# The first mixer's and the memory's products as single fp32 matmuls, without high and low parts

## The chip, the cores and the metric

The kernel runs on one core of one Trainium2 chip. The metric is the device time of one execution in microseconds (us). The core's engines are TensorE (PE, with its weight loads as PEld), VectorE (DVE), ScalarE (ACT), GpSimd (POOL) and SyncE (SP), which here issues the DMAs. Each works through its own queue in order and waits on semaphores for the others. TensorE's clock has two levels, 1.2 and 2.4 GHz; the profile gives the granted clock as a share of the full one.

## What is computed

A decoder trunk of two layers on 512 tokens of width 1024, in fp32. Layer 0's mixer ("mixer A") scores earlier keys with a light indexer, keeps the top 128 of them for each query, and attends to these. In both layers four more heads attend to 256 memory tokens.

```python
proj = rms_norm(x, norm_mix) @ w_in            # q, k, v, qi, ki, wi, qm of mixer A
logits = einsum('bqhd,bsd->bqhs', qi, ki)
score = einsum('bqhs,bqh->bqs', relu(logits), wi)
_, idx = top_k(score, n_sel)                   # n_sel = 128
# softmax attention of q over the kept k, v (12 query heads, 4 key heads, rotary)
kv = rms_norm(mem, norm_mem) @ w_mem_kv        # both layers
# softmax attention of qm over the memory's keys and values
x = x + concat([mix, mo]) @ w_out
x = x + swiglu_ffn(rms_norm(x, norm_ffn))
```

Layer 1 has another mixer (dilated windows), and a final norm ends the kernel.

## The kernel before

Activations lie transposed, 128 features by 512 tokens to a tile, eight such tiles (KT = 8) for the width of 1024. A product takes a weight tile of 128 output columns and accumulates eight matmuls of 128x128 weights by 512 tokens in one PSUM bank.

Each of the large products is made in three parts. The operands are split into a high part in fp32r, a format of reduced precision, and a low part, the rest (`_split2`, L48 on ACT and L51 on DVE or POOL). For each k there are three matmuls: high by high, low by high, high by low (`projs` L225 to L227, `proj_steps` L213 to L215, `token_major` L403 to L405 for values, which lie token by token in 256 columns, `scores` L414 for the attention's score products, which take 64 rows a head and so run a pair of heads in the two halves of the array). The weights come through `load` (L176) into `wf`, a ring of two buffers of 1 MB with two weight tiles each; `wsplit` makes `wh` and `wl` of them (three buffers each), so that a `wf` buffer is free as soon as its tiles are split. `prep` (L309, L310) makes the split input `xh`, `xl`. Small products are plain fp32: `row` (L268) spreads the reciprocal roots along the tokens, `pv` (L385) multiplies probabilities by values with the two heads of a pair in the two column halves of the array, and the transposes (L427).

Only PE's order is written by hand, in the order of the code; a scheduler orders the other engines when the program is built, and that order is fixed. `layer0` issues on PE: the indexer's key and first query tile together, three more index queries, then (woven, `_weave`) the first key tile and the values with the index logits of four head pairs and three query blocks each; then the memory's row, the second key tile, two memory queries, the memory's keys and values (`memory_kv`), memory attention woven with four query tiles, and the sparse attention in 18 units, into which the last two query tiles, layer 1's memory products (`memory_ahead`) and the output projection are filled. The logits go through ReLU on ACT into SBUF (L756) and are summed up on DVE (L758, L760). The top-k (`topk`) is sixteen rounds on DVE, each with a maximum (L695) and a replacement (L696) for three query blocks, and masks at the end (L700). Memory attention reduces its scores on DVE (L555), which ACT's exponential then needs. The memory's squares are summed on POOL (`memory_squares`, L282, L294); `ssq_cols` and `rsqrt_cols` (L234 to L243, a chain of thirteen small DVE steps) make the reciprocal roots of them, and `row` spreads these (DVE L266, PE L268).

```python
for k in range(KT):                                     # proj_steps, before
    s = slice(k * 128, (k + 1) * 128)
    mm(out, wh[:, s], xh[k], start=k == 0, stop=False)
    mm(out, wh[:, s], xl[k], start=False, stop=False)
    mm(out, wl[:, s], xh[k], start=False, stop=k == KT - 1)
```

## Time and profile before

| | us |
|---|---|
| median of 3 timed runs | 1280.42 (1276.65 to 1281.71) |
| profiled execution | 1287.35 |
| its span, first to last instruction | 1285.6 |
| PE busy | 1218.7 (95%) |
| weight loads (PEld) busy | 983.7 (77%) |
| DVE busy | 586.0 (46%) |
| ACT busy | 498.7 (39%) |
| POOL busy | 389.4 (30%) |
| mean granted TensorE clock | 0.973 |

The profiled execution is one of its own, a little longer than the median. By the chain of work that ended last, PE holds 81% of the span and DVE 12%. A busy share is an average over stages with different limits: the feed-forward parts, which fill most of the span, keep PE busy almost without a gap, while the first quarter of the span has many. A record's duration includes the way through the array, so the pace of matmuls is read from one start to the next.

### The profile page before, as it was taken

How to read it: one execution, taken by the hardware profiler on the slowest of the kernel's cores; microseconds unless marked ns; L12 is line 12 of the kernel's file. 1: busy time of each engine (PE TensorE's matmuls, PEld its weight loads, DVE VectorE, ACT ScalarE, POOL GpSimd, SP SyncE). 2: the span in 40 equal slices, each digit the busy share in tenths (PEclk: the TensorE clock that was granted, in tenths of full speed). 3: DMA queues.
4: the chain of work that ended last, by engine and by line, in shares of the span. 5: the costliest groups of instructions: out<-in, count | busy, mean ns of one | idle time of the engine just before them, and what ended most of it. 6: DMA issues, size and time to landing. Idle time of an engine off the chain costs nothing.

```text
span 1285.6 us, 14958 instructions
## 1 busy us (share of the span) xinstructions
PE 1218.7 (95%) x5868; PEld 983.7 (77%) x5868; DVE 586.0 (46%) x1054; ACT 498.7 (39%) x859; POOL 389.4 (30%) x242
## 2 busy tenths in 40 slices
PE   6688979999999999999998999999999999999997
PEld 5467657677888888888886779887788888888886
DVE  7789976548333333322224542548533333331212
ACT  6564666525323322322223764534332233222222
POOL 4637464244222122212222322333322221121222
PEclk9789999999999999999998999989899999999998
DMA  5402132212222222222233111211222222222221
GB/s 179 131 33 101 49 113 72 70 36 97 78 88 97 98 99 98 78 90 90 90 111 107 66 66 34 97 35 41 92 98 89 80 94 98 99 90 90 91 90 66
DMA packets 30214, 109.98 MB, mean 86 GB/s; under 512 B 2495, under 2 KB 12095, under 8 KB 21695
## 3 DMA queue, kind: packets, MB, share of 16 engines
q1 hardware_dynamic: 29598, 108.50, 24.1%
q8 instruction: 46, 0.75, 0.2%
q10 hardware_dynamic: 544, 0.52, 0.1%
q14 instruction: 26, 0.20, 0.0%
HBM read 105.74 MB, written 3.28 MB: 85 GB/s over the span
## 4 chain that ended last, share of the span: by engine, by line
PE 81%; DVE 12%; DMA 3%; issue 1%; ACT 1%; POOL 1%; SPq 0%; DVEq 0%; ACTq 0%; POOLq 0%
PE psS L226 5%; PE psS L225 5%; PE psS L227 5%; PE psT L225 3%; PE psT L227 3%; PE psT L226 3%; PE psacc L225 3%; PE psacc L226 3%; PE psacc L227 3%; PE psacc L200 3%; PE psS L414 3%; PE psS L200 3%; PE psS L202 3%; PE psS L201 3%; PE psacc L202 3%; PE psacc L201 3%
## 5 line engine op out<-in xcount | busy, mean ns | idle before, releaser
L51 POOL TENSOR_TENSOR wl<-wf,wh 128x1024 fp32r<-128x1024 f32 x98 | 238.5, 2434 | 684.6 <-ACT wh L48 621.8
L48 ACT CAST wh<-wf 128x1024 fp32r<-128x1024 f32 (+1 forms) x178 | 183.6, 1032 | 527.9 <-issue 171.3
L51 DVE TENSOR_TENSOR wl<-wf,wh 128x1024 fp32r<-128x1024 f32 (+1 forms) x95 | 118.5, 1247 | 94.1 <-ACT wh L48 94.1
L225 PE MATMUL psS<-xh,wh 128*128 128x512 f32 x296 | 120.0, 405 | 6.8 <-ACT wh L48 6.8
L227 PE MATMUL psS<-xh,wl 128*128 128x512 f32 x296 | 119.2, 403 | 2.8 <-DVE wl L51 2.8
L226 PE MATMUL psS<-xl,wh 128*128 128x512 f32 x296 | 118.9, 402 | 2.8 <-DVE xl L310 2.8
L225 PE MATMUL psT<-xh,wh 128*128 128x512 f32 x200 | 81.1, 405 | 0.0
L227 PE MATMUL psT<-xh,wl 128*128 128x512 f32 x200 | 80.7, 403 | 0.0
L226 PE MATMUL psT<-xl,wh 128*128 128x512 f32 x200 | 80.7, 403 | 0.0
L225 PE MATMUL psacc<-xh,wh 128*128 128x512 f32 x192 | 77.3, 403 | 0.0
L226 PE MATMUL psacc<-xl,wh 128*128 128x512 f32 x192 | 76.9, 401 | 0.0
L227 PE MATMUL psacc<-xh,wl 128*128 128x512 f32 x192 | 76.9, 400 | 0.0
L225 PEld LDWEIGHTS psS<-xh,wh 128*128 128x128 f32 x296 | 56.8, 192 | 20.5 <-ACT wh L48 6.8
L227 PEld LDWEIGHTS psS<-xh,wl 128*128 128x128 f32 x296 | 56.7, 191 | 17.2 <-DVE wl L51 4.2
L226 PEld LDWEIGHTS psS<-xl,wh 128*128 128x128 f32 x296 | 56.8, 192 | 16.7 <-DVE xl L310 3.3
L294 POOL TENSOR_TENSOR ssq<-ssq,t 128x512 f32<-128x512 f32 (+1 forms) x34 | 50.8, 1493 | 55.1 <-ACT t L284 53.9
L213 PE MATMUL psacc<-xh,wh 128*128 128x512 f32 x144 | 62.9, 437 | 0.0
L652 DVE TENSOR_TENSOR raw<-psacc,R 128x512 f32<-128x512 f32 x22 | 15.2, 691 | 103.1 <-PE psacc L227 103.1
L215 PE MATMUL psacc<-xh,wl 128*128 128x512 f32 x144 | 58.1, 404 | 0.0
L214 PE MATMUL psacc<-xl,wh 128*128 128x512 f32 x144 | 58.0, 403 | 0.0
L339 POOL TENSOR_TENSOR raw<-raw,table 128x512 f32<-128x512 f32 x21 | 26.9, 1283 | 72.7 <-ACT raw L336 54.9
L627 DVE TENSOR_TENSOR xT<-xT,psacc 128x512 f32<-128x512 f32 x44 | 30.1, 686 | 38.7 <-PE psacc L202 38.6
(335 smaller groups left out, 2812.7 us busy)
## 6 DMA issues: line engine op xcount, KB each, us to landing
wf<-in_gu SPq DMA_DIRECT2D x44, 1024.0 KB
wf<-in_dn SPq DMA_DIRECT2D x16, 1024.0 KB
wf<-in_in SPq DMA_DIRECT2D x13, 1024.0 KB
wf<-in_dn SPq DMA_DIRECT2D x16, 384.0 KB
wf<-in_v SPq DMA_DIRECT2D x3, 1024.0 KB
xT<-in_x SPq DMA_DIRECT2D x8, 256.0 KB
wf<-in_mk SPq DMA_DIRECT2D x2, 1024.0 KB
wf<-in_mv SPq DMA_DIRECT2D x2, 1024.0 KB
```

The source lines that it names most:

```text
L48: nc.scalar.copy(hi, src)
L51: lo_engine.tensor_tensor(out=lo, in0=src, in1=hi.bitcast(F32), op=ALU.subtract)
L200: mm(out, wh[k], xh[k], start=first and k == 0, stop=False)
L201: mm(out, wh[k], xl[k], start=False, stop=False)
L202: mm(out, wl[k], xh[k], start=False, stop=last and k == n - 1)
L213: mm(out, wh[:, s], xh[k], start=k == 0, stop=False)
L214: mm(out, wh[:, s], xl[k], start=False, stop=False)
L215: mm(out, wl[:, s], xh[k], start=False, stop=k == KT - 1)
L225: mm(out, wh[:, s], xh[k], start=k == 0, stop=False)
L226: mm(out, wh[:, s], xl[k], start=False, stop=False)
L227: mm(out, wl[:, s], xh[k], start=False, stop=k == KT - 1)
L294: engine.tensor_tensor(out=parts[part], in0=parts[part], in1=sq, op=ALU.add)
```

## The change

- The input of the first mixer is scaled once on DVE (`scaled`), without a split; the memory is scaled once on ACT (`memory_scaled`). The weights are used straight from `wf` (`plain_chunks`, and `load` alone for values). The products of the first mixer, except its output projection, and the memory's products of both layers take one fp32 matmul for each k (`fp32_steps`, `fp32_tokens`).
- Index queries and keys, queries, keys and memory queries and keys are kept whole, so their score products take one fp32 matmul a head instead of three in fp32r. `rope` and `plain` no longer split their result; in `rope_steps` POOL now does the multiplications.
- ReLU of the logits is done in place in PSUM, and the logits use the banks of two tags in turn.
- `angles` moves behind the first products. `memory_squares` moves behind the first key step, and `ssq_cols` of the memory behind the logits and values. `row` of the memory and its scaling move behind the second key tile.
- `memory_ahead` uses the memory that is still in SBUF and doesn't load it again; what it keeps in DRAM for layer 1 is halved for the keys.

```diff
+    def plain_chunks(self, name, order):
+        src = self.io[name]
+        for a in range(0, len(order), 2):
+            m = min(2, len(order) - a)
+            w = self.load(src[order[a]:order[a] + m].rearrange("t p n -> p t n"), [m, KT * 128])
+            for j in range(m):
+                yield w[:, j]
+    def fp32_steps(self, out, w, x):
+        for k in range(KT):
+            self.nc.tensor.matmul(out, w[:, k * 128:(k + 1) * 128], x[k], start=k == 0, stop=k == KT - 1)
+            if k % 2:
+                yield 1
+    def fp32_tokens(self, out, w, ks, x, b):
+        n = out.shape[-1]
+        for k in ks:
+            self.nc.tensor.matmul(out, x[k][:, b], w[:, k * n:(k + 1) * n], start=k == 0, stop=k == KT - 1)
...
+    def scaled(self, gi):
+        ...
+            nc.vector.tensor_scalar(t, self.xT[:, k], self.gains[:, gi, k:k + 1], None, op0=ALU.mult)
+            add(self.xT[:, k], 0, nc.vector)
...
         mm = self.nc.tensor.matmul
+        if units[0][2] is None:
+            for out, q, _, k, _, rows, qs, ks in units:
+                mm(out, q[rows, qs], k[rows, ks], start=True, stop=True)
+            return
         for a in range(3):
...
     def layer0(self):
-        self.angles()
-        xh, xl, parts = self.prep(0, early=4, squares=(1, 3))
-        first = [self.wsplit(self.first[j], nc.vector) for j in range(2)]
+        x, parts = self.scaled(0)
...
         cols = self.ssq_cols(parts)
+        self.angles()
...
         index_q(1, p1)
-        mem_parts = self.memory_squares(mem)
...
-                ps = [self.psum("S") for _ in range(2)]
-                self.scores([(ps[s][:, :n], qih, qil, kih, kil, slice(s * 64, s * 64 + 64), q, slice(0, n))
+                tag = ("S", "acc")[(j + i) % 2]
+                ps = [self.psum(tag) for _ in range(2)]
+                self.scores([(ps[s][:, :n], qi, None, ki, None, slice(s * 64, s * 64 + 64), q, slice(0, n))
                              for s in range(2)])
                 for s in range(2):
-                    t = self.tmp(("t", "o")[s])
+                    t = ps[s]
-                    self.mark = nc.scalar.activation(t[:, :n], ps[s][:, :n], AF.Relu)
+                    nc.scalar.activation(t[:, :n], t[:, :n], AF.Relu)
...
-        def rope_steps(dst, *out, tag="acc", mul=None):
+        def rope_steps(dst, out, tag="acc"):
             p = self.psum(tag)
-            yield from self.proj_steps(p, next(ws), xh, xl)
-            dst.append(self.rope(p, cs, sn, *out, add=nc.gpsimd, split=nc.gpsimd, mul=mul))
+            yield from self.fp32_steps(p, next(ws), x)
+            dst.append(self.rope(p, cs, sn, out, None, add=nc.gpsimd, mul=nc.gpsimd))
...
         next(steps)
-        self.mem_cols = self.ssq_cols(mem_parts, n=2, keep=True)
+        mem_parts = self.memory_squares(mem)
         every = itertools.chain.from_iterable(logits(j) for j in range(4))
         _weave(itertools.islice(steps, 12), every, nb=1)
-        self.mem_row = self.row(self.mem_cols, 2, dst=self.cst.tile([128, MEM], F32, name="mem_row"))
-        mem = self.memory_split(0, mem)
         for _ in steps:
             pass
-        for _ in rope_steps(K, kb[:, 2], kb[:, 3], tag="T", mul=nc.gpsimd):
+        self.mem_cols = self.ssq_cols(mem_parts, n=2, keep=True)
+        for _ in rope_steps(K, kb[:, 1], tag="T"):
             pass
+        self.mem_row = self.row(self.mem_cols, 2, dst=self.cst.tile([128, MEM], F32, name="mem_row"))
+        xm = self.memory_scaled(0, mem)
```

The change also moves instructions. In the rows that follow a line number is that of the kernel the rows are from.

PE before, in the first key tile's steps, ahead of the first logits: the matmul of the memory's squares (`ssq`), from which the reciprocal roots come, stands between two of the key's matmuls (`psO`).

```order
L214 MATMUL psO<-xl,wh 128x512
L215 MATMUL psO<-xh,wl 128x512
L256 MATMUL psacc<-ones,ssq 128x2 x2
L213 MATMUL psO<-xh,wh 128x512
```

PE now, from the last logits (`ki`, `qi`) to the first scores of memory attention (`km`, `qm`): `xg` is the scaled input, `mg` the scaled memory.

```order
L440 MATMUL psacc<-ki,qi 128x384 x2
L440 MATMUL psS<-ki,qi 128x512 x2
L278 MATMUL psacc<-ones,ssq 128x2 x2
L207 MATMUL psT<-xg,wf 128x512 x8
L290 MATMUL psacc<-raw,ones 128x256
L207 MATMUL psacc<-xg,wf 128x512 x16
L207 MATMUL psacc<-mg,wf 128x256 x16
L215 MATMUL psacc<-wf,mg 128x256 x16
L440 MATMUL psS<-km,qm 128x256 x4
```

The matmul of the squares moved behind the last logits, and only the second key tile (x8) now stands between it and the row's matmul (L290).

DVE before, in the first logits' sums: the last steps of the memory's reciprocal roots (`rs_q`, `rs_keep`) and the multiplication that makes the row's operand of them (L266).

```order
L242 SCALAR_TENSOR_TENSOR rs_q<-rs_v,rs_q 128x2
L758 TENSOR_SCALAR score<-t,wi 128x256
L243 SCALAR_TENSOR_TENSOR rs_keep<-rs_q,rs_keep 128x2
L760 SCALAR_TENSOR_TENSOR score<-o,wi,score 128x256
L758 TENSOR_SCALAR score<-t,wi 128x384
L760 SCALAR_TENSOR_TENSOR score<-o,wi,score 128x384
L340 TENSOR_TENSOR raw<-raw 128x512
L333 TENSOR_TENSOR raw<-psO,table 128x512
L266 TENSOR_SCALAR raw<-ident,rs_keep 128x128 x2
```

DVE now, behind the last logits' sums: the same chain, with the first top-k round (`m_` are its maxima).

```order
L261 TENSOR_SCALAR rs_keep<-rs_i 128x2
L263 TENSOR_TENSOR rs_q<-rs_keep 128x2
L709 MAX m_900<-score 128x8
L709 MAX m_903<-score 128x8
L709 MAX m_906<-score 128x8
L264 SCALAR_TENSOR_TENSOR rs_q<-rs_v,rs_q 128x2
L710 MATCH_REPLACE score<-m_900,score 128x512
L710 MATCH_REPLACE score<-m_903,score 128x384
L710 MATCH_REPLACE score<-m_906,score 128x256
L265 SCALAR_TENSOR_TENSOR rs_keep<-rs_q,rs_keep 128x2
```

And DVE now, where the chain ends: the row's operand (L288) in the fifth round.

```order
L265 SCALAR_TENSOR_TENSOR rs_keep<-rs_q,rs_keep 128x2
L709 MAX m_936<-score 128x8
L709 MAX m_939<-score 128x8
L709 MAX m_942<-score 128x8
L288 TENSOR_SCALAR raw<-ident,rs_keep 128x128 x2
L710 MATCH_REPLACE score<-m_936,score 128x512
```

The chain moved from among the logits to among the top-k, where four rounds and three maxima stand ahead of its end.

DVE before, in the middle of the top-k: two reductions of memory attention (L555) stand between the maxima of one round.

```order
L695 MAX m_1545<-score 128x8
L555 TENSOR_REDUCE nm<-psS 128x2 x2
L695 MAX m_1548<-score 128x8
L695 MAX m_1551<-score 128x8
L127 TENSOR_SCALAR o<-o 128x128
L696 MATCH_REPLACE score<-m_1545,score 128x512
```

DVE now, at the end of the top-k: the last round's replacements, the masks (L714), and then the first reductions (L569).

```order
L710 MATCH_REPLACE score<-m_1035,score 128x512
L710 MATCH_REPLACE score<-m_1038,score 128x384
L710 MATCH_REPLACE score<-m_1041,score 128x256
L714 TENSOR_SCALAR score<-score 128x512
L714 TENSOR_SCALAR score<-score 128x384
L714 TENSOR_SCALAR score<-score 128x256
L569 TENSOR_REDUCE nm<-psS 128x2 x4
L486 RECIPROCAL den<-den 128x8
L449 COPY pt<-psT 128x2x256 x2
```

All reductions of memory attention moved from within the top-k to behind it.

## Rows read from the trace of the kernel before

**Rows 1.** By stage: length, PE, PEld, DVE, ACT, POOL busy, clock, DMA share, GB/s
```profile
0.00:48.43 48.43, 36.27 (x134) 27.65 (x135) 33.13 (x53) 27.49 (x43) 20.46 (x17) 0.96 0.53 173
48.43:96.71 48.28, 34.88 (x197) 26.37 (x196) 42.86 (x62) 29.23 (x58) 27.67 (x22) 0.79 0.16 56
96.71:131.15 34.44, 30.36 (x172) 26.83 (x171) 33.83 (x82) 14.39 (x22) 23.88 (x19) 0.95 0.33 121
131.15:171.20 40.05, 36.97 (x201) 25.97 (x200) 40.05 (x102) 25.59 (x60) 22.68 (x15) 1.00 0.14 45
171.20:301.89 130.69, 121.70 (x721) 90.82 (x721) 78.93 (x190) 68.90 (x173) 57.15 (x38) 0.97 0.20 70
```

**Rows 2.** Timeline, PE: start, us, operation, records [idle before, releaser]; fp32 among fp32r
```profile
318.66 1.02 PE L268 MATMUL psacc<-raw,ones 128*128 128x512 f32 x2
319.12 0.79 PE L225 MATMUL psS<-xh,wh 128*128 128x512 f32 x1
319.75 0.40 PE L226 MATMUL psS<-xl,wh 128*128 128x512 f32 x1
319.98 0.40 PE L227 MATMUL psS<-xh,wl 128*128 128x512 f32 x1
```

**Rows 3.** Timeline, PE: products of 256 columns in fp32r
```profile
214.32 0.28 PE L404 MATMUL psacc<-wh,ml 128*128 128x256 f32 x1
214.44 0.28 PE L405 MATMUL psacc<-wl,mh 128*128 128x256 f32 x1
```

**Rows 4.** Timeline, PE: fp32 on column halves; a pair of scores and what follows
```profile
146.49 1.94 PE L385 MATMUL psO<-pt,vm 128*64 128x512 f32 x8
...
217.69 0.50 PE L414 MATMUL psS<-k,qh 64*128 64x512 f32 x2
...
218.59 1.73 PE L385 MATMUL psO<-pt,v 128*64 128x512 f32 x8
```

**Rows 5.** Timeline, PE: waits of the first two stages
```profile
6.83 0.79 PE L225 MATMUL psS<-xh,wh 128*128 128x512 f32 x1 [6.83 <-ACT wh L48]
...
12.47 0.79 PE L227 MATMUL psS<-xh,wl 128*128 128x512 f32 x1 [2.02 <-DVE wl L51]
...
34.28 1.12 PE L268 MATMUL psacc<-raw,ones 128*128 128x512 f32 x2 [2.56 <-DVE raw L266]
...
59.58 1.01 PE L256 MATMUL psacc<-ones,ssq 128*128 128x2 f32 x4 [9.61 <-POOL ssq L294]
```

**Rows 6.** Timeline, SP: issues of two weight loads
```profile
37.28 1.31 SPq L176 DMA_DIRECT2D wf<-in_vw  x1
...
95.39 0.37 SPq L176 DMA_DIRECT2D wf<-in_mk  x1
```

**Rows 7.** Timeline, ACT: the value weights' first use
```profile
48.20 1.05 ACT L48 CAST wh<-wf 128x1024 fp32r<-128x1024 f32 x1 [0.69 <-DMA wf<-in_vw]
```

**Rows 8.** Timeline, POOL: first of the memory's squares; the first table behind them
```profile
43.64 0.61 POOL L282 TENSOR_TENSOR ssq<-mem 128x256 f32<-128x256 f32 x1 [11.74 <-DMA mem<-in_mem]
...
59.48 1.74 POOL L373 TENSOR_TENSOR table<-raw,R 128x512 f32<-128x512 f32 x1
```

**Rows 9.** Timeline, DVE: two rounds of the top-k, a memory key, the masks
```profile
101.61 1.48 DVE L695 MAX8 m<-score 128x8 f32<-128x512 f32 x3 [0.40 <-POOL score L762]
...
104.59 1.47 DVE L695 MAX8 m<-score 128x8 f32<-128x512 f32 x3
...
119.62 0.42 DVE L362 SCALAR_TENSOR_TENSOR t<-psacc,mem_row 128x256 f32<-128x256 f32 x1
...
167.90 4.22 DVE L700 TENSOR_SCALAR score<-score 128x512 f32<-128x512 f32 x3
```

**Rows 10.** Timeline, DVE: one of the reciprocal root's small steps
```profile
32.16 0.16 DVE L241 TENSOR_TENSOR rs_q<-rs_y 128x4 f32<-128x4 f32 x1
```

**Rows 11.** Short stretches, columns as in rows 1: after a stop; during a load
```profile
60.00:66.00 6.00, 6.00 (x19) 4.45 (x20) 5.30 (x6) 3.59 (x7) 6.00 (x5) 0.50 0.27 70
...
96.00:100.00 4.00, 4.00 (x19) 3.04 (x20) 3.90 (x4) 1.50 (x4) 3.20 (x3) 1.00 0.71 265
```

More of the change, by code (lines that the diff above doesn't have):

```diff
@@ L315, in prep @@
         return xh, xl, parts
-    def rope_proj(self, w, xh, xl, cs, sn, hi, lo, any_bank=False, by_residue=False):
-        p = self.psum_any() if any_bank else self.psum("acc")
-        self.proj(p, w, xh, xl)
-        return self.rope(p, cs, sn, hi, lo, by_residue)
+    def scaled(self, gi):
+        nc = self.nc
+        xg = []
+        add, parts = self.squares()
+        for k in range(KT):
+            if k % 4 == 0:
+                big = self.big("xg", F32)
+            t = big[:, (k % 4) * S:(k % 4 + 1) * S]
+            nc.vector.tensor_scalar(t, self.xT[:, k], self.gains[:, gi, k:k + 1], None, op0=ALU.mult)
+            add(self.xT[:, k], 0, nc.vector)
+            xg.append(t)
+        return xg, parts
     def rope(self, p, cs, sn, hi, lo, by_residue=False, mul=None, add=None, split=None, twice=None):
@@ L339, in rope @@
         (mul or nc.gpsimd).tensor_tensor(out=sw, in0=sw, in1=sn, op=ALU.mult)
-        (add or nc.vector).tensor_tensor(out=raw, in0=raw, in1=sw, op=ALU.add)
+        last = hi if lo is None and twice is None else raw
+        (add or nc.vector).tensor_tensor(out=last, in0=raw, in1=sw, op=ALU.add)
         if twice is not None:
-            nc.vector.tensor_tensor(out=raw, in0=raw, in1=twice, op=ALU.mult)
+            nc.vector.tensor_tensor(out=hi, in0=raw, in1=twice, op=ALU.mult)
+        if lo is None:
+            return hi
         if by_residue:
@@ L514, in memory_ahead @@
+            t = self.slot("vm", F32)[:, :256]
+            self.values(p, self.mem_cols[:, i:i + 1], t)
+            yield t
+    def memory_ahead(self, mem):
         nc = self.nc
-        mem = self.load(self.io["mem"].rearrange("(k p) n -> p k n", p=128), [KT, MEM])
-        m = self.memory_split(1, [mem[:, k] for k in range(KT)])
-        self.kept = self.dram.tile([4, 128, 512], F32, name="kept")
+        x = self.memory_scaled(1, mem)
+        self.kept = self.dram.tile([4, 128, 256], F32, name="kept")
@@ L518, in memory_ahead @@
         n = 0
-        for r in self.memory_kv(1, m):
-            if r:
-                n_cols = 512 if n < 2 else 256
-                nc.sync.dma_start(self.kept[n][:, :n_cols], r[1].bitcast(F32)[:, :n_cols])
+        for r in self.memory_kv(1, x):
+            if r is not None:
+                nc.sync.dma_start(self.kept[n], r)
                 n += 1
@@ L526, in memory_back @@
     def memory_back(self):
-        ts = []
-        for n in range(4):
-            ts.append(self.slot("kept", F32R if n < 2 else F32))
-            n_cols = 512 if n < 2 else 256
-            self.nc.sync.dma_start(ts[n].bitcast(F32)[:, :n_cols], self.kept[n][:, :n_cols])
-        self.mem_kv = [(t[:, :MEM], t[:, MEM:]) for t in ts[:2]], ts[2:]
+        ts = [self.slot("kept", F32)[:, :256] for _ in range(4)]
+        for n, t in enumerate(ts):
+            self.nc.sync.dma_start(t, self.kept[n])
+        self.mem_kv = ts[:2], ts[2:]
     def memory_attention(self, qm, early):
@@ L703, in layer0 @@
         nc, mm = self.nc, self.nc.tensor.matmul
-        self.angles()
-        xh, xl, parts = self.prep(0, early=4, squares=(1, 3))
-        first = [self.wsplit(self.first[j], nc.vector) for j in range(2)]
+        x, parts = self.scaled(0)
         pk, pq = self.psum("S"), self.psum("S")
-        self.projs([(pk, first[0]), (pq, first[1])], xh, xl)
-        ws = itertools.chain(self.chunks("in0", [2, 3]), self.chunks("in0", [4, 5]),
-                             self.chunks("in0", list(range(6, 15)), lo=("gpsimd", "gpsimd")))
+        for k in range(KT):
+            for p, w in zip((pk, pq), self.first):
+                mm(p, w[:, k * 128:(k + 1) * 128], x[k], start=k == 0, stop=k == KT - 1)
+        ws = itertools.chain(self.plain_chunks("in0", [2, 3]), self.plain_chunks("in0", [4, 5]),
+                             self.plain_chunks("in0", list(range(6, 15))))
         def product(tag="T"):
             p = self.psum(tag)
-            self.proj(p, next(ws), xh, xl)
+            for _ in self.fp32_steps(p, next(ws), x):
+                pass
             return p
         cols = self.ssq_cols(parts)
+        self.angles()
         ci, si = (self.angle_table(1, sine, self.slot("table", F32)) for sine in (False, True))
@@ L873, in layer0 @@
         outs = list(self.mem_out)
-        fill = itertools.chain(queries(2), self.memory_ahead())
+        fill = itertools.chain(queries(2), self.memory_ahead(mem))
         for u in range(-ahead, nu + 4):
```

98 lines of the change are left out of this document (34 added, 64 removed).

## Prediction

> **What bounds the kernel now.** I read the table by stage first, then PE's timeline inside the first stages for its waits, then DVE's and POOL's timelines for who ends them. The change touches only the first mixer (the first 301.89 us of the span) and layer 1's short memory attention, so five stages matter: A to 48.43 (indexer products), B to 96.71 (index logits woven with key and value products), C to 131.15 (second keys, memory queries, memory's keys and values), D to 171.20 (memory attention woven with four queries), E to 301.89 (sparse attention) [rows 1]. In A and B PE stands idle or at low clock: in B it is busy 34.88 of 48.28 us at a mean granted clock of 0.79. In C and D it is DVE that is full: 33.83 of 34.44 us and 40.05 of 40.05; that is the top-k, with everything else threaded through it. E is PE's. So the change has to be costed on PE in A, B and E, and on DVE's queue in C and D.
>
> **What one product costs.** Before, a product of 512 columns is three matmuls 0.23 us apart, 0.70 us. The trace holds plain fp32 matmuls too: the one that spreads a row enters PE at 318.66 as two records; the next matmul's record is stretched (0.79 instead of 0.40 us), and the one after starts at 319.75, so its own place was 319.75 - 0.23 = 319.52 [rows 2]. A plain fp32 product therefore takes 0.86 us, 0.16 more than the three it replaces. At 256 columns three at 0.115 us are 0.35 [rows 3]; half of 0.86 is 0.43: 0.08 more. So the change makes PE's work longer and takes work from ACT, DVE and POOL.
>
> Score products of 64 rows go in pairs, one head in each half of the array. A pair at 512 columns takes 0.90 us with three passes; eight fp32 records of 512 columns on the two column halves take 1.94 us, where four products one by one would take 3.44, so fp32 runs two at a time there [rows 4]. No fp32 product on row halves is shown. Lower bound: two at a time, one pass more, +0.23 us per 512 columns; upper bound: one head after the other, a further 0.86. In units of 512 columns B has 9 pairs (4 x (256+384+512)), D 4, E 15, layer 1 another 4. I take the lower bound, since the halves of the other kind are the nearest row: +2.1, +0.9, +3.5, +0.9 us.
>
> The Trainium skill (Perfetto Trace Analysis, Engine Utilization) halves TensorE's rate for FP32_LOW_HIGH; read as the price of a whole product, that would be 0.47 us and a saving. The row shows each of the two records at half rate, so the trace agrees by record and not by product; by the rule the time would be that of the first rival.
>
> **Stage A.** Five products of eight: 40 x 0.16 = +6.4. The first product no longer waits for the weight's cast (1.0 us), the next not for its low part (2.02), and the reciprocal root no longer for a DVE that splits (2.56) [rows 5]; the low clock that follows costs half of (1 - 0.96) x 2 x 48.43 = 3.9 us, 1.9. The load of tiles 4 and 5 now waits until the first products are through with their buffer, and stands behind the memory loads on SP; the load that stood there before was issued at 37.28 and used at 48.20 [rows 6, 7]. I give it 1.3. Sum +0.2.
>
> **Stage B.** The 13.4 us of idle go: 9.61 of them wait for the memory's squares [rows 5], whose product moves behind the logits. B's work at full clock is 24 x 0.23 + 96 x 0.115 + logits 9 x 0.90 + 1.0 for small ones = 25.6 us against 34.88 busy, so slow clock is another 9.3. New work: 8 x 0.16 + 32 x 0.08 = 3.8, logits 2.1. New waits: index query 3 is multiplied on POOL behind the fifteen memory squares and two tables (43.64 to 59.48 us for the squares alone, perhaps 7 us earlier now [rows 8]), and its sum on DVE stands ahead of the first logit's: PE comes to the third logit some 4 us early. A wait for the last banks (1.5) and slow clock after them (2). 48.28 - 13.4 - 9.3 + 5.9 + 7.5 = 39.0: -9.3.
>
> **Stage C, where the sign is decided.** Call T0 the moment when PE's matmul for the memory's root stands behind the last logits. In DVE's new order the root's steps alternate with top-k rounds, and the row product's operand comes after four rounds and three maxima (order rows in the section on the change). A round takes 104.59 - 101.61 = 2.98 us [rows 9], a root step 0.2 [rows 10]. So: 2.5 for the last logits on ACT, DVE and POOL, 4 x 2.98 + 1.4 + 9 x 0.2 + 0.4 = 15.5: the operand is there at T0 + 18. PE has 8 x 0.86 = 6.9 us of second keys for that time and then stands for 10.8 us; behind the waiting matmul all its queue stands, the memory queries first. Then: 0.3, memory queries 16 x 0.86 = 13.8, slow clock after the stop 2.5 (after the 9.6 us stop 60 to 66 us ran at 0.50 [rows 11]), memory keys 16 x 0.43 = 6.9. The memory's value weights take the key weights' buffer, because the other holds a query tile still to come; formerly the split copies freed it early, now only the last product does. A load of 1 MB issued at 95.39 had moved by 100 [rows 6, 11]: 4.9 with the issue, and 1.7 of slow clock; values 6.9. Together T0 + 55.
>
> DVE says the same by itself: in its new order all sixteen rounds stand ahead of the first reduction of memory attention. 2.5 + 16 x 2.98 + 13 x 0.2 + 0.4 + 0.8 + the three masks: T0 + 55 if these take 1.2 us without POOL beside them, T0 + 58 at the 4.2 us they took [rows 9]. The two memory keys' multiplications are the 0.8 (0.42 each) [rows 9]. Even if PE's stops vanished, memory attention could not start earlier. C: 55 - 34.4 = +20.6, bounds +17 and +25. Formerly C and D overlapped with the top-k; now D follows it.
>
> **Stage D.** 32 x 0.16 = 5.1 and scores 0.9; DVE is free, so 2 of the 3.1 us of idle go: +4.0. **Stage E.** Queries 16 x 0.16 = 2.6, layer 1's memory products 32 x 0.08 = 2.6, scores 3.5; 5 of 9.0 us of idle go (the memory's low parts and casts no longer stand on DVE), and 2 of slow clock (0.97): +1.7. **Layer 1** scores +0.9, less splitting of its memory queries hidden under PE: +0.9. The two feed-forward parts and layer 1's products stay as they are.
>
> **Sum.** +0.2 - 9.3 + 20.6 + 4.0 + 1.7 + 0.9 = +18.1. The profiled execution took 1287.35 us (span 1285.6), so 1305.5 by its own time; the three timed runs have a median of 1280.42, and I forecast 1280.4 + 18.1 = 1299 us rounded up, 1.4% slower. Errors of some 4 us in B, C and E each give the forecast itself about 1284 to 1314.
>
> **Rivals.**
> - *Faster: the two records of a product follow at fp32r's pace (0.47 us).* Against the forecast a product of 512 columns is then 0.39 cheaper, one of 256 0.20, a score pair 0.46. A: 40 x 0.39 = 15.6, of which the load of tiles 4 and 5 holds some 12 back, so -3.7. B: 3.1 + 6.4 + 4.1, of which the POOL chain holds 5 back, so -18. C keeps its +20.6, since DVE's queue sets it. D: 12.5 + 1.8, so -10. E: 6.2 + 6.4 + 6.9, so -18. Layer 1 -1. Sum -30: 1250. The row at 318.66 speaks against it [rows 2]. A, B, D and E hold 96 products of 512 and 64 of 256 columns, so it takes the sign from 0.86 - 18.1 / 128 = 0.72 us a product downwards. Chance 0.06.
> - *No change: C keeps its length.* If the root's steps and memory attention's reductions got through while the top-k runs, C would stay near 35 and the sum be -2.5: 1278. DVE's queue runs in its order and the order is fixed at build, which speaks against it; that logits could end earlier than I sum them speaks for it. Chance 0.10.
> - *Slower still: fp32 score pairs on row halves run one head after the other.* 32 x 0.86 = +27.5: 1326. Column halves speak against it; nothing shows it excluded. Chance 0.12.
> - That the change doesn't do what it says: the splits are gone from ACT, DVE and POOL by the order, so no chance is kept for it.
>
> **How the numbers follow.** The forecast has 0.70, other causes 0.02. A measurement tells about 0.5%, 6.4 us, from no change. Of the forecast's 0.70 about 0.09 lies within that. Slower 0.61 + 0.12 = 0.73; same 0.10 + 0.09 = 0.19; faster 0.06 + 0.02 = 0.08. The range reaches from the no-change rival with its error (1277) to just past the score rival (1328); left out are the first rival and the tails, about 0.15.
>
> **What would show it.** In the profile after: two records per product 0.43 us apart (0.86 a product); DVE full with the top-k without a break, PE idle by 8 to 13 us before the memory's row product and about 5 before the memory's value products, the first reduction of memory attention behind the masks; B shorter by about 8 us. It is wrong if the row product doesn't wait, if a product takes 0.70 us or less, or if B ends as late as before.

## Result and the profile after

The changed kernel takes 1297.06 us (median of 4 runs, 1296.31 to 1298.61) against 1280.45 us (4 runs, 1276.65 to 1281.71): a ratio of 1.0136, 95% interval 1.0113 to 1.0159. It is slower by 1.4%, as forecast (1299). The profiled execution took 1297.15 us, span 1295.4. Of the kernels below, one execution each of *root_early* (1731.91 us) and *late_split_relu_sbuf* (1707.64 us) ran at a mean granted clock of 0.65 and is left out of their medians.

By stretch, in the profiled executions (before: [rows 1]; "rest" is everything from the first feed-forward product on):

| stretch | before | forecast | after | difference |
|---|---|---|---|---|
| A | 48.43 | +0.2 | 46.91 | -1.5 |
| B | 48.28 | -9.3 | 40.49 | -7.8 |
| C | 34.44 | +20.6 | 56.13 | +21.7 |
| D | 40.05 | +4.0 | 43.62 | +3.6 |
| E | 130.69 | +1.7 | 132.03 | +1.3 |
| first mixer | 301.89 | +17.2 | 319.18 | +17.3 |
| rest | 983.7 | +0.9 | 976.2 | -7.5 |

The rest hardly changed in the code. The profiled execution of before was 6.9 us above its median, and 4.4 of the 7.5 us lie in the first feed-forward part (last section). The same stages after, columns as in [rows 1]:

```profile
0.00:46.91 46.91, 40.05 (x95) 17.74 (x95) 22.40 (x56) 16.99 (x29) 11.74 (x20) 1.00 0.56 186
46.91:87.40 40.49, 36.67 (x130) 19.69 (x128) 20.35 (x37) 22.71 (x49) 10.79 (x12) 0.92 0.11 35
87.40:143.53 56.13, 40.25 (x119) 24.05 (x119) 53.97 (x166) 5.58 (x11) 6.92 (x7) 0.85 0.15 53
143.53:187.15 43.62, 41.93 (x153) 19.74 (x153) 9.58 (x16) 22.48 (x57) 15.14 (x13) 1.00 0.18 61
187.15:319.18 132.03, 126.48 (x626) 83.33 (x625) 64.33 (x170) 65.54 (x170) 48.31 (x32) 1.00 0.20 68
```

In the third row DVE is busy 53.97 of 56.13 us and PE only 40.25; in the fourth DVE has 9.58 us of work left, where before it had 40.05. The top-k no longer lies beside memory attention but ahead of it. PE's timeline of the changed kernel (start, us, operation, records, idle before and its releaser) has every wait that the forecast named:

```profile
31.64 7.03 PE L207 MATMUL psT<-xg,wf 128*128 128x512 f32 x16
39.94 7.13 PE L207 MATMUL psT<-xg,wf 128*128 128x512 f32 x16 [0.92 <-DMA wf<-in_in]
59.19 2.54 PE L440 MATMUL psacc<-ki,qi 64*128 64x512 f32 x4 [3.38 <-DVE score L774]
71.33 1.13 PE L440 MATMUL psS<-ki,qi 64*128 64x512 f32 x4
72.39 1.78 PE L215 MATMUL psT<-wf,xg 128*128 128x256 f32 x7
87.40 0.58 PE L278 MATMUL psacc<-ones,ssq 128*128 128x2 f32 x4 [0.44 <-DVE score L776]
87.84 7.11 PE L207 MATMUL psT<-xg,wf 128*128 128x512 f32 x16
105.91 1.22 PE L290 MATMUL psacc<-raw,ones 128*128 128x256 f32 x2 [10.96 <-DVE raw L288]
106.93 16.01 PE L207 MATMUL psacc<-xg,wf 128*128 128x512 f32 x32
122.77 7.07 PE L207 MATMUL psacc<-mg,wf 128*128 128x256 f32 x32
134.76 1.76 PE L215 MATMUL psacc<-wf,mg 128*128 128x256 f32 x4 [4.92 <-DVE score L710]
143.53 1.13 PE L440 MATMUL psS<-km,qm 64*128 64x256 f32 x8
```

A product is two records: the 16 of an index query's tile, in stretch A, stand from 31.64 to 38.60, 0.87 us a product. A score pair of 512 columns takes 72.39 - 71.33 = 1.06 us, so the two heads run side by side. T0, PE's matmul for the memory's root, is 87.40: the row's product stood 10.96 us and the memory's values 4.92 us, and memory attention began at T0 + 56.1.

DVE's timeline of the same kernel: the row's operand, the masks at the end of the top-k, the first reduction of memory attention.

```profile
105.40 0.46 DVE L288 TENSOR_SCALAR raw<-ident,rs_keep 128x128 f32<-128x128 f32 x2
...
140.59 0.88 DVE L714 TENSOR_SCALAR score<-score 128x512 f32<-128x512 f32 x3
144.69 1.29 DVE L569 TENSOR_REDUCE nm<-psS 128x2 f32<-128x512 f32 x2 [3.21 <-PE psS L440]
```

The top-k was through at T0 + 54.1 and DVE then waited 3.21 us for PE. Two limits of nearly the same length stand here, PE's chain of stops and DVE's block of rounds; PE's was the longer by these 3.21 us. The experiments take them apart.

### The profile page after: what moved, and what is told of

Its sections match the earlier page's. It is cut to its first block, busy times and chain, and to the rows that moved or that the text cites. A ratio compares the mean times of both kernels' runs of the same rounds, so it can differ in the third digit from the quotient of the medians.

```text
span 1295.4 us, 14141 instructions
## 1 busy us (share of the span) xinstructions
PE 1237.4 (96%) x5548; PEld 947.0 (73%) x5548; DVE 526.3 (41%) x1010; ACT 465.2 (36%) x818; POOL 330.6 (26%) x218
## 4 chain that ended last, share of the span: by engine, by line
PE 83%; DVE 8%; DMA 3%; ACT 2%; POOL 1%; issue 1%; SPq 0%; DVEq 0%; ACTq 0%; POOLq 0%
PE psS L248 5%; PE psS L249 5%; PE psS L247 5%; PE psacc L207 3%; PE psT L248 3%; PE psT L249 3%; PE psT L247 3%; PE psacc L248 3%; PE psacc L249 3%; PE psacc L247 3%; PE psacc L222 3%; PE psS L222 3%; PE psS L224 3%; PE psS L223 3%; PE psacc L224 3%; PE psacc L223 3%
## 5 line engine op out<-in xcount | busy, mean ns | idle before, releaser
L51 POOL TENSOR_TENSOR wl<-wf,wh 128x1024 fp32r<-128x1024 f32 x82 | 197.9, 2413 | 658.6 <-ACT wh L48 588.2
L48 ACT CAST wh<-wf 128x1024 fp32r<-128x1024 f32 x153 | 157.3, 1028 | 507.0 <-issue 167.0
L51 DVE TENSOR_TENSOR wl<-wf,wh 128x1024 fp32r<-128x1024 f32 x86 | 103.0, 1197 | 89.6 <-ACT wh L48 89.6
L247 PE MATMUL psS<-xh,wh 128*128 128x512 f32 x272 | 107.7, 396 | 0.0
L249 PE MATMUL psacc<-xh,wl 128*128 128x512 f32 x176 | 70.3, 400 | 0.0
L248 PE MATMUL psacc<-xl,wh 128*128 128x512 f32 x176 | 70.3, 399 | 0.0
L247 PE MATMUL psacc<-xh,wh 128*128 128x512 f32 x176 | 70.2, 399 | 0.0
L207 PE MATMUL psacc<-xg,wf 128*128 128x512 f32 x128 | 61.1, 619 | 0.0
L207 PEld LDWEIGHTS psacc<-xg,wf 128*128 128x128 f32 x128 | 23.8, 196 | 29.0 <-issue 28.8
L367 ACT COPY raw<-psacc 32x512 f32<-32x512 f32 x72 | 41.6, 577 | 4.4 <-DVE raw L364 3.3
L235 PE MATMUL psacc<-xh,wh 128*128 128x512 f32 x96 | 41.1, 428 | 0.0
```

Of the source, the lines that this page charges most:

```text
L48: nc.scalar.copy(hi, src)
L51: lo_engine.tensor_tensor(out=lo, in0=src, in1=hi.bitcast(F32), op=ALU.subtract)
L207: self.nc.tensor.matmul(out, w[:, k * 128:(k + 1) * 128], x[k], start=k == 0, stop=k == KT - 1)
L367: nc.scalar.copy(sw[a:a + 32], p[b:b + 32])
```

## Experiments

Times are medians, ratios are to runs of the kernel before on the same chip.

**1. PE's stops, one by one and together.** *root_early* moves the memory's root ahead of the last head pair's logits, *values_early* regroups the loads, *root_values_early* does both.

```diff
-        every = itertools.chain.from_iterable(logits(j) for j in range(4))
+        def root():
+            self.mem_cols = self.ssq_cols(mem_parts, n=2, keep=True)
+            yield from logits(3)
+        every = itertools.chain(logits(0), logits(1), logits(2), root())
...
-        self.mem_cols = self.ssq_cols(mem_parts, n=2, keep=True)
```

```diff
-                             self.plain_chunks("in0", list(range(6, 15))))
+                             self.plain_chunks("in0", [6]), self.plain_chunks("in0", list(range(7, 15))))
```

> The changed kernel with one edit: the matmul of the memory's squares and the reciprocal roots stand ahead of the last head pair's logits instead of behind all of them. The row's operand then stands behind two top-k rounds on DVE instead of four, and the first reductions of memory attention in the sixteenth round. Theory (two limits that lie close together: PE's stops and DVE's block of top-k rounds): the stop before the row's product shrinks from 10.96 us to some 2.5, so PE could begin memory attention 45 us after the last logits, but the first reduction comes only at 2.5 + 15 x 2.98 + 1.4 + 1.2 = 50 us instead of 57.3; gain 7.5, about 1289.5. Rival 1 (PE's stop alone sets the length): the whole stop of 8.5 us and 2.5 us of slow clock come back, 1286, and no wait of PE for a reduction appears. Rival 2 (DVE's block alone sets it): 1295 to 1297, and the stop turns up again before the second scores.

> The changed kernel with one edit: the second key's weight tile is loaded alone and the two memory queries' tiles together, so that the memory's value weights can be loaded while the memory's keys are multiplied. Theory: the wait of 4.92 us before the memory's value products is one for that load, and goes, with the 1.7 us of slow clock behind it. DVE's top-k block ended 3.2 us before the first reduction, and the first reductions now stand ahead of the last maxima and the masks, some 3 us more, so nearly all of it comes back: 4 to 6 us, 1291 to 1293. Rival (that wait is one for DVE, as the page's releaser says, and not for the load): no change, 1297, and the idle time stands where it stood.

> Both edits together: the memory's root ahead of the last head pair's logits, and the value weights' load earlier. DVE's order, fixed at build, now has the first reductions in the thirteenth round. Theory (both stops and the order of DVE together make the longer stretch): PE could begin memory attention 39 us after the last logits, the first reduction is due at 2.5 + 12 x 2.98 + 1.4 + 1.2 = 41 us instead of 57.3: gain 16, 1281. Rival (DVE's top-k has to end before memory attention whatever its place): 1291 or more.

> The kernel of root_early once more, for its profile (there the clock was low all through). It came out at 1294, 2.7 us below the changed kernel, where 7.5 were expected. Theory (the top-k block on DVE holds what the stop gives): PE reaches the first scores some 8 us earlier than 143.5, and then stands for the first reduction, which comes at 140 or later. Rival: PE reaches the scores no earlier, because the stop before the row or the one before the value products has grown.

| kernel | us | ratio, 95% | first scores | first reduction | mixer's end |
|---|---|---|---|---|---|
| changed | 1297.06 | 1.0136 (1.0113 to 1.0159) | 143.53 | 144.69 | 319.18 |
| root_early | 1292.23 | 1.0111 (1.0074 to 1.0147) | 136.68 | 138.90 | 317.55 |
| values_early | 1296.69 | 1.0133 (1.0095 to 1.0171) | 135.84 | 139.83 | 318.00 |
| both | 1282.03 | 1.0034 (1.0016 to 1.0052) | 124.58 | 128.52 | 306.71 |

The stages of root_early are read from *root_early_again*, one more execution of the same kernel (1301.05 us). PE's timelines of root_early_again, values_early and root_values_early:

```profile
98.39 1.22 PE L290 MATMUL psacc<-raw,ones 128*128 128x256 f32 x2 [2.93 <-DVE raw L288]
...
127.62 9.13 PE L215 MATMUL psacc<-wf,mg 128*128 128x256 f32 x32 [4.96 <-DMA wf<-in_mv]
...
142.02 1.13 PE L440 MATMUL psS<-km,qm 64*128 64x256 f32 x6 [1.67 <-ACT raw L573]
```

```profile
128.84 7.07 PE L215 MATMUL psacc<-wf,mg 128*128 128x256 f32 x32
135.84 1.13 PE L440 MATMUL psS<-km,qm 64*128 64x256 f32 x8
...
142.96 1.13 PE L440 MATMUL psS<-km,qm 64*128 64x256 f32 x6 [3.44 <-ACT raw L573]
```

```profile
96.41 0.70 PE L290 MATMUL psacc<-raw,ones 128*128 128x256 f32 x2 [2.92 <-DVE raw L288]
...
117.58 7.07 PE L215 MATMUL psacc<-wf,mg 128*128 128x256 f32 x32
124.58 1.13 PE L440 MATMUL psS<-km,qm 64*128 64x256 f32 x8
```

In root_early the stop before the row shrank from 10.96 to 2.93 us, and in values_early there is no idle time before the value products. In root_early_again, where that wait still stands, its releaser is named as their load, so the releaser in the changed kernel's row (DVE) was the wrong one. But each edit alone gave little. values_early began the scores 7.7 us earlier and the reduction only 4.9; PE stood 3.44 us behind it, for ACT's exponential, and the sparse attention began 3.2 us earlier. Its expectation (4 to 6 us) missed. root_early's first reduction came when expected (50 us after the logits), and the sparse attention began 5.8 us earlier, but E took 4.2 us longer in that profile, at a granted clock of 0.97 instead of 1.00. Of the 7.5 us expected the timed runs show 3.2 by the ratios and 4.8 between the medians.

Together the edits gave 13 us by the ratios (15 between the medians) where the two gains alone add up to 3.6 (5.2); at the mixer's end the profiles have 12.5 us against 1.6 and 1.2. This is as expected (1281). With both, DVE's order has the first reductions in the thirteenth round, in root_early and values_early in the sixteenth. The order is built anew for each kernel; that it follows from PE coming earlier in the scheduler's reckoning is likely, but no run shows it. So the loss in C was neither the stops nor the block alone but both, one behind the other's cover.

**2. The order alone, in the kernel before.** *before_root_late* moves the memory's squares, root, row and split as the change does, and nothing else.

```diff
-        mem_parts = self.memory_squares(mem)
...
-        self.mem_cols = self.ssq_cols(mem_parts, n=2, keep=True)
+        mem_parts = self.memory_squares(mem)
...
         for _ in steps:
             pass
+        self.mem_cols = self.ssq_cols(mem_parts, n=2, keep=True)
         for _ in rope_steps(K, kb[:, 2], kb[:, 3], tag="T", mul=nc.gpsimd):
             pass
+        self.mem_row = self.row(self.mem_cols, 2, dst=self.cst.tile([128, MEM], F32, name="mem_row"))
+        mem = self.memory_split(0, mem)
```

> The kernel before with one part of the change alone: the memory's squares behind the first key step, their roots behind the logits, the row and the split memory behind the second key; all products stay in three fp32r matmuls. In DVE's order the row's operand stands behind four top-k rounds, as in the changed kernel. Theory (the loss of the stretch behind the logits comes from this order, not from the fp32 products): the stretch to the end of the logits loses its stop of 9.6 us, some 10 us in all, and the one behind it gains a stop of some 12: net +2, between 1278 and 1288. Rival (the fp32 products make the loss, the order costs nothing): 1270.

1294.94 us, ratio 1.0119 (1.0079 to 1.0160): the order alone costs about as much as the whole change. The rival (1270) is out, and the theory's 1278 to 1288 missed too, because B did not gain. C took 47.18 us, 12.7 more than before, much as expected (some 12). The other parts of the change then add 8.9 us in C, 1.6 in D and 2.4 in E, and take 1.5 in A and 6.9 in B. PE's timeline of this kernel, the stops among the logits and before the row:

```profile
56.50 0.58 PE L414 MATMUL psS<-kil,qih 64*128 64x256 f32 x2 [3.33 <-DVE kil L51]
64.36 0.69 PE L414 MATMUL psS<-kih,qih 64*128 64x384 f32 x1 [3.81 <-ACT t L755]
73.05 0.38 PE L414 MATMUL psS<-kih,qih 64*128 64x256 f32 x1 [1.93 <-ACT t L755]
...
116.00 1.22 PE L268 MATMUL psacc<-raw,ones 128*128 128x256 f32 x2 [14.19 <-DVE raw L266]
```

Its stretch B, columns as in [rows 1]:

```profile
48.40:95.80 47.40, 34.28 (x195) 25.54 (x193) 37.45 (x48) 29.22 (x58) 28.38 (x23) 0.82 0.17 57
```

The stop of 9.61 us for the squares [rows 5] is gone, the first logits start at 51.09 instead of 63.29, and the last at 95.27 instead of 96.39: new waits took it all. PE's waits in B add up to 13.1 us, 8.5 for ReLU on ACT and 4.6 for split operands on DVE, against 13.4 before and 3.8 in the changed kernel. The row then stood 14.19 us. So in the split kernel the stop hid other waits of the same length, and the move alone shortens nothing. B became shorter only with the rest of the change. That this is the splits' absence is likely (ACT is busy for 22.71 us in B after the change, for 29.22 here), but the logits also got the banks of a second tag, and no run takes these two apart.

**3. ReLU.** *relu_sbuf* is the changed kernel with ReLU written to SBUF again.

```diff
-                    t = ps[s]
+                    t = self.tmp(("t", "o")[s])
-                    nc.scalar.activation(t[:, :n], t[:, :n], AF.Relu)
+                    nc.scalar.activation(t[:, :n], ps[s][:, :n], AF.Relu)
```

> The changed kernel with ReLU of the logits written to SBUF, as before, instead of in place in PSUM. Theory (the stop of 3.38 us before the third block of logits is the chain of the last index query on POOL and DVE, not the banks): banks come free at ACT instead of DVE, so PE doesn't stop there, but the sums still stand behind that chain; the logits end at most 2 us earlier or later and the time is 1295 to 1298. Rival (in-place ReLU holds the banks and costs the stop): the logits end 3.4 us earlier, 1293 to 1294.

1292.24 us, 1.0123 (1.0081 to 1.0165), which the timed runs can't tell from the changed kernel's. The trace can: PE's timeline has no stop before the third block of logits,

```profile
56.06 0.92 PE L440 MATMUL psS<-ki,qi 64*128 64x384 f32 x4
58.82 1.13 PE L440 MATMUL psacc<-ki,qi 64*128 64x512 f32 x4
```

and the last logits start at 82.16 instead of 86.37. From the first logits to the last it takes 28.65 us instead of 35.93: the stop is gone, and the granted clock, 0.51 from 60 to 67 us behind the stop in the changed kernel, is 1.00 here. The logits end about as the rival said and the time is below both forecasts, but the banks are not shown to be the reason, because the build also ordered DVE differently. ACT and DVE of the changed kernel:

```profile
51.36 2.34 ACT L367 COPY raw<-psT 32x512 f32<-32x512 f32 x4 [11.74 <-DVE raw L364]
```

```profile
50.43 0.29 DVE L130 TENSOR_TENSOR strided<-o 128x128 bf16<-128x128 f32 x1
50.64 0.69 DVE L364 TENSOR_TENSOR raw<-psT,table 128x512 f32<-128x512 f32 x1
...
58.65 0.48 DVE L774 TENSOR_SCALAR score<-psacc,wi 128x256 f32<-128x256 f32 x1
```

DVE makes the attention masks (L114 to L130) from 46.12 on, after a wait of 4.67 us for POOL's squares, and ahead of an index query's step (L364) for which ACT then idles 11.74 us. The masks work in the temporary tiles `t` and `o`, which ReLU into SBUF takes as well, and in relu_sbuf they stand behind the logits, from 83.77 on. There the same step starts at 43.90 and the first sum at 56.66, 2.2 us before PE comes to the third block, so with ReLU in place PE would hardly have stood there either. In the changed kernel PE did wait for the bank until DVE's first sum; whether the bank or the masks' place made the 3.38 us is open. *late_split* below and its kernel with ReLU in SBUF differ in the same two things (a stop of 1.70 us and none). Of the 4.2 us, 1.6 went into the stop before the row (12.57 us), and 2.8 were left when the scores began.

**4. What fp32 costs where nothing waits.** *plain_row_early* takes both edits of 1, puts the root ahead of the last two head pairs' logits, and the row ahead of the second key. *late_split* is the same with the input split beside the top-k, behind the last logits, and with the six queries and the sparse scores in three fp32r matmuls.

```diff
-        for _ in rope_steps(K, kb[:, 1], tag="T"):
+        self.mem_row = self.row(self.mem_cols, 2, dst=self.cst.tile([128, MEM], F32, name="mem_row"))
+        for _ in rope_steps(K, kb[:, 1], tag="T"):
```

```diff
+        wq = self.chunks("in0", list(range(9, 15)), lo=("gpsimd", "gpsimd"))
...
-            yield from self.fp32_steps(p, next(ws), x)
+            yield from self.proj_steps(p, next(wq), xh, xl) if xh else self.fp32_steps(p, next(ws), x)
...
+        for k in range(KT):
...
+            cast = nc.scalar.copy(bh[:, t], x[k])
+            low = nc.gpsimd.tensor_tensor(out=bl[:, t], in0=x[k], in1=bh[:, t].bitcast(F32), op=ALU.subtract)
+            for late, first in ((cast, self.mark), (low, self.sel)):
+                self.tc.add_manual_dep(late.ins, first.ins.name, mybir.DependencyInfo(
+                    mybir.DependencyClass.NoSync, mybir.DependencyReason.DATA), reason="order")
```

> The changed kernel with single fp32 products throughout, the value weights' load early, the memory's root ahead of the last two head pairs' logits, and its row ahead of the second key. Nothing of PE's stops is left behind the logits but the reductions: theory: memory attention begins at 122 us instead of 124.6 (the stop of 2.92 before the row goes), the first reduction is due in DVE's thirteenth round at some 127 us, 1.5 earlier than 128.5: 1279 to 1281. The rest against the mixed kernel, some 10 us, is then the price of fp32 products where nothing waits: 24 of 512 and 32 of 256 columns and 4 score units up to memory attention, 32 products beside it, 16 and 32 and 15 score units later, 21 us of PE time in all, less what splitting costs there. Rival (the fp32 products cost nothing there): the two kernels are within 3 us.

> The kernel of plain_row_early, single fp32 products up to memory attention, but with the six queries and the sparse attention's scores in three fp32r matmuls again; the input is split on ACT and POOL only behind the last logits, beside the top-k, where these engines are nearly idle. Theory (what the mixed kernels lost among the logits, 5 to 6 us, was the split of the input there): the logits end at 86 to 87 us, memory attention begins 36 us later as in plain_row_early, and the stretches behind it take 40 to 44 and 131 us instead of 47 and 134: 1270 to 1274, against 1281 for plain_row_early and 1274 for mixed_dve. Rival (POOL's subtractions beside the top-k slow DVE, or the queries wait for their weights' low parts): 1277 or more.

> The same with ReLU of the logits in SBUF. Theory (the banks come free at ACT, PE no longer stops for DVE's late sums, and the stretch behind follows PE, not the top-k): the logits end at 82 to 83 us, and 3 us of it stay: 1267 to 1271. Rival (the first reduction of memory attention stands in DVE's thirteenth round, and the top-k begins only when the sums are done: nothing is left): the same time as the kernel with ReLU in PSUM, within 1 us.

plain_row_early: 1281.4 us, 1.0021 (0.9997 to 1.0045); the scores began at 122.51 and the first reduction at 127.12, as expected. With the order mended the change is neither gain nor loss that these runs can tell. Against mixed (experiment 5) it is 5 us longer, where some 10 were expected, because mixed itself came out too long. late_split: 1266.89 us, 0.9891 (0.9858 to 0.9925), and with ReLU in SBUF (*late_split_relu_sbuf*) 1263.71 us, 0.9879 (0.9845 to 0.9913): both beat both kernels, by more than expected; the timed runs can't tell the two apart. The stretches C, D and E, columns as in [rows 1], of plain_row_early and of late_split:

```profile
87.20:122.51 35.31, 35.22 (x115) 21.50 (x115) 34.71 (x103) 5.75 (x11) 6.93 (x7) 1.00 0.33 115
122.51:169.97 47.46, 43.63 (x154) 20.48 (x153) 25.35 (x67) 22.80 (x57) 15.16 (x13) 0.96 0.13 45
169.97:303.80 133.83, 128.17 (x626) 83.59 (x625) 64.33 (x170) 65.68 (x170) 48.33 (x32) 0.99 0.20 67
```

```profile
89.20:124.35 35.15, 35.15 (x115) 21.43 (x115) 34.65 (x102) 12.27 (x22) 18.93 (x17) 1.00 0.32 116
124.35:166.35 42.00, 38.00 (x185) 26.62 (x185) 27.28 (x70) 26.21 (x60) 24.03 (x16) 0.96 0.23 81
166.35:291.52 125.17, 121.73 (x689) 89.58 (x689) 66.76 (x173) 65.91 (x171) 52.26 (x36) 1.00 0.18 62
```

C is the same work and the same length; 12 us more on POOL beside the top-k cost nothing. The logits of late_split ended 2 us later than expected. In D four queries cost 5.5 us more as fp32 products (the forecast's price gives 32 x 0.16 = 5.1). In E two queries and fifteen score units cost 8.7 us against plain_row_early, whose granted clock was 0.99 there, and 6.9 against the changed kernel (132.03), which ran at 1.00 like late_split (forecast 6.1). E of late_split differs from E of before (130.69) mainly by layer 1's memory products, which stay single (689 PE records instead of 721); it is 5.5 us shorter, so that part of the change pays.

**5. Splitting the input among the logits.** *mixed* is the changed kernel up to the logits and the kernel before behind them, with the root early; its input is split as soon as ACT and POOL have room. *mixed_dve* makes the low parts on DVE, *mixed_dve_relu_sbuf* also puts ReLU in SBUF.

```diff
+        for k in range(KT):
...
+            _split2(nc, bh[:, t], bl[:, t], x[k], nc.gpsimd)
```

```diff
-            _split2(nc, bh[:, t], bl[:, t], x[k], nc.gpsimd)
+            _split2(nc, bh[:, t], bl[:, t], x[k], nc.vector)
```

> The changed kernel up to the end of the logits, the kernel before behind them: index products, first key, values and index scores stay single fp32 matmuls; the input is split behind that, and the second key, memory queries, memory's keys and values, queries and all attention scores are three fp32r matmuls again. The memory's root stands ahead of the last two head pairs' logits, and the row's operand ahead of the top-k. Theory (unsplit products pay where PE waited for splits, and cost where it doesn't): the logits end near 87 us as in the changed kernel, and the three stretches behind them take 34 to 35, 40 and 130 us as in the kernel before: the feed-forward part begins at 291 to 293 us instead of 301.89, and the time is 1268 to 1271, 0.7% below the kernel before. Rival (the splitting of the input among the logits and of the weights beside the top-k takes the gain back on ACT, POOL and DVE): 1278 or more.

> The mixed kernel with one edit: the low parts of the input, which POOL made without a break for 9.88 us, are made on DVE. In the mixed kernel the small steps of the memory's root on DVE took 1.2 us each while POOL worked, and 0.16 us after it, and PE stood 6.06 us for a sum behind them. Theory (the small steps are slow because POOL works beside them): most of the steps take 0.16 to 0.3 us again, the stop of 6.06 us falls below 2, the logits end near 88 us instead of 92.6, and the time is 1271 to 1273. Rival (the steps are slow for another reason, or the eight subtractions of 0.7 us in DVE's queue cost as much): the logits end at 92 or later, 1276 or more.

> The same with ReLU of the logits in SBUF again. Theory (in place, a bank stays taken until DVE has summed it, and DVE is late; to SBUF it comes free at ACT): the logits end another 3 to 4 us earlier, at 84 to 85 us, and since the stretches behind them no longer depend on the top-k alone, half of it or more stays: 1268 to 1271. Rival (what the logits win, DVE's queue of sums gives back before the top-k): within 1 us of the kernel with ReLU in PSUM.

mixed: 1276.35 us, 0.9985 (0.9967 to 1.0004), between its theory (1268 to 1271) and its rival (1278 or more). C, D and E took 34.2, 39.8 and 131.3 us, as expected; the logits ended 5 us too late (last at 92.61), which is where the gain went. DVE's timeline of mixed has the memory's root while POOL subtracts, and after POOL is done (POOL's row below; a subtraction of weights follows it until 80.92):

```profile
76.23 1.19 DVE L279 SCALAR_TENSOR_TENSOR rs_keep<-rs_q,rs_keep 128x2 f32<-128x2 f32 x1
77.45 1.19 DVE L277 TENSOR_TENSOR rs_q<-rs_keep 128x2 f32<-128x2 f32 x1
...
81.17 0.16 DVE L277 TENSOR_TENSOR rs_q<-rs_keep 128x2 f32<-128x2 f32 x1
```

```profile
68.74 9.88 POOL L51 TENSOR_TENSOR xl<-xg,xh 128x512 fp32r<-128x512 f32 x8
```

mixed_dve: 1274.3 us, 0.9970 (0.9950 to 0.9990). The steps took 0.15 to 0.17 us again except one of 2.21 us, beside which POOL made a low part of weights; this bears the theory out. But the last logits still started at 91.78, nearly as late as the rival said, since the first four subtractions took 5.51 us in DVE's queue ahead of the sums. The time lies between theory (1271 to 1273) and rival (1276 or more). mixed_dve_relu_sbuf: 1277.04 us, 0.9992 (0.9973 to 1.0011); its expectation missed, PE stood 6.87 us for the root behind the same subtractions. late_split, which splits the input behind the logits, came to 1266.89; it also keeps the second key's, the memory queries' and the memory's products single, so the difference is not the place of the split alone.

## Why the prediction was right, and where it was not

- **Prices.** 0.86 us a product was forecast, 0.87 measured; +0.23 for a score pair, measured 1.06 - 0.90 = +0.16. The faster rival (0.47 us) and the slower one (heads one after the other) are refuted by the two rows of PE above. The Trainium skill (Perfetto Trace Analysis, Engine Utilization) halves TensorE's rate for FP32_LOW_HIGH; the trace agrees for each of a product's two records, not for the product.
- **C (+20.6, measured +21.7).** The stop before the row (10.8, measured 10.96), the load (4.9, measured 4.92) and DVE's block (T0 + 55 to 58, measured T0 + 54.1) all came within 1 us; DVE was a little early because the masks at the end of the top-k took 0.88 us. The statement that without PE's stops memory attention could not start earlier is wrong in two ways. In the order as built DVE stood 3.21 us for PE, so that much was PE's. And the sentence held DVE's order fixed, while every edit gets an order of its own: with both stops shortened the reductions came in the thirteenth round, and memory attention began 18.9 us earlier.
- **B (-9.3, measured -7.8): right size, wrong reason.** The step that failed put 9.61 us of it down to the stop for the squares. Experiment 2 moved the squares without touching the products, and the last logits started only 1.1 us earlier. The gain needs the rest of the change, most likely the missing splits; whether it needs the move as well is open, because no run has single products with the squares in their old place. The 4 us before the third logit (measured 3.38) were laid to query 3's chain on POOL and DVE. PE did wait for DVE there, but DVE was late for the masks too, which the forecast did not have, and what the bank in PSUM adds is open (experiment 3).
- **A (+0.2, measured -1.5).** Of the 1.7 us between them, 0.4 are the load of tiles 4 and 5, which cost 0.92 and not 1.3, and 0.8 are a second wait for a low part before, which the sum left out (PE's row of before below); the other 0.5 are not traced.

```profile
8.80 0.80 PE L227 MATMUL psS<-xh,wl 128*128 128x512 f32 x1 [0.76 <-DVE wl L51]
```

- **D (+4.0, measured +3.6) and E (+1.7, measured +1.3).** The sums came out, but not every term of E: by experiment 4 two queries and fifteen score units cost 6.9 us at equal clock where 6.1 were put down, and the memory's part gave 5.5 where 4.4 were (2.6 for its products, less 5 of idle time and 2 of slow clock). The two errors nearly cancel.
- **The time.** The mixer's shift of 17.3 against 17.2 forecast, and 16.6 between the medians. That so many terms came out within 2 us is partly luck: B's gain had the wrong cause, and E's errors cancel.
- **The no-change rival** (C keeps its length) is the one that an engineer can bring about: root_values_early comes near that kernel, with 38.75 us in C, at 1282.03 (1278 forecast).

## What to carry to other kernels

When an edit changes number formats and moves a step as well, time the move alone in the old kernel: here the move alone cost as much as the whole change, and with the order mended the change was even. Unsplit products came with a gain in the stretches where PE had waited for splits (the first 90 us here) and mostly cost where it had not, so decide stage by stage, and put the split where its engines are idle. Two limits of equal length hide each other: removing either shows little alone, so remove both before calling either harmless. And look at the built order of the other engines after every edit: moving ReLU also moved the masks.

## What the hardware showed that was not expected

**Small DVE steps beside POOL.** A step on 128x2 elements takes 0.16 us alone and 1.19 us while POOL runs tensor-by-tensor work (mixed, above). In the changed kernel, too, with POOL's row behind:

```profile
98.29 1.04 DVE L265 SCALAR_TENSOR_TENSOR rs_keep<-rs_q,rs_keep 128x2 f32<-128x2 f32 x1
...
100.84 0.14 DVE L263 TENSOR_TENSOR rs_q<-rs_keep 128x2 f32<-128x2 f32 x1
```

```profile
98.06 1.26 POOL L370 TENSOR_TENSOR raw<-raw,table 128x512 f32<-128x512 f32 x1 [1.10 <-ACT raw L367]
```

The step that started at 98.29, beside POOL's multiplication, ended with it, at 99.3. The trace of before has such steps as well (1.21 us each at 63.61, 64.85 and 66.09), while the forecast took 0.2 for every step. By 0.16 and 1.19 us a step a root of thirteen such steps takes 2 us or 15 us (an estimate), depending on what POOL does. The maxima of the top-k are not slowed: beside POOL's subtractions, in late_split_relu_sbuf, three took 1.48 us, as in [rows 9].

**Two paces at the full granted clock.** Three-part products back to back, PE records in 50 us (columns: length, PE busy and records, granted clock, DMA share, GB/s), in the execution of before and in the one of after:

```profile
340.00:390.00 50.00, 50.00 (x216) 1.00 0.30 106
...
620.00:670.00 50.00, 50.00 (x220) 1.00 0.27 101
```

```profile
340.00:390.00 50.00, 50.00 (x220) 1.00 0.23 85
...
940.00:990.00 50.00, 50.00 (x216) 1.00 0.25 90
```

The pace changes by 1.9% within one execution and from one to the next, with the clock shown at 1.00 in all four rows; what sets it stays open. In the first feed-forward part, from its first weight load to the load at 552.70 before and 565.61 after, it comes to 4.4 of the 7.5 us in the rest (250.65 us against 246.29). The other 3 us come later and are not explained. It is why stretches of two profiles should be compared to a per cent or two only, and small differences by many timed runs.
